# A hybrid encoder layer on one core: two query groups head by head, stick-breaking weights as differences, and masking inside a scan

## The chip, the cores and the metric

The kernel runs on one core of a Trainium2 chip. The time is the device time of one execution in microseconds (us); before the change it is 2670.81 us, the median of three runs from 2665.74 to 2673.22. Engines are called as in the profile: PE (TensorE, with PEld for its weight loads), DVE (VectorE), ACT (ScalarE), POOL (GpSimd) and SP, whose queue starts nearly all DMA transfers.

## The reference

One layer: an RMS norm with scale and shift, one input projection, two kinds of attention with eight heads of 64 channels each, an output projection, and an MLP of 1024 x 4096 with a squared ReLU. The sequence has 2048 positions, the model 1024 channels, all float32. The change touches the stick-breaking heads most:

```python
z = jnp.einsum('bqhd,bkhd->bhqk', qb, kb).astype(jnp.float32) * scale
strict = s_idx < t_idx
log_beta = jax.nn.log_sigmoid(z)
log_1m_beta = jnp.where(strict, jax.nn.log_sigmoid(-z), 0.0)
suffix = lax.cumsum(log_1m_beta, axis=3, reverse=True) - log_1m_beta
w = jnp.where(strict, jnp.exp(log_beta + suffix), 0.0)
out = jnp.einsum('bhqk,bkhd->bqhd', w.astype(v.dtype), vb)
```

So the weight of a key is sigmoid(z) times the product of sigmoid(-z) over all keys between it and the query. The other eight heads are a softmax over the query's chunk of 64 and the eight chunks before it, with a relative bias:

```python
s = jnp.einsum('bnqhd,bnkhd->bnhqk', qc, k_band) * (d ** -0.5) + bias[None, None]
p = jax.nn.softmax(jnp.where(valid[None, :, None, None, :], s, NEG_INF), axis=-1)
```

## The kernel before

The sequence is reversed on the host, so that a key before a query stands to its right and the product over keys runs from left to right. Positions are cut into four blocks of 512, numbered 0 to 3; block 3 holds the earliest positions. Nearly all matrices are split into a high and a low part of float32r, and a product is made of two or three matmuls of these.

There are three stages. The first, some 420 us, normalizes and projects what the attention needs first, and puts q, k and v into DRAM scratch. The last, from about 1370 us, is the end of the output projection and the MLP. Between them lies the attention stage. It is a list of *units* (`units`), each of four steps. A unit `SB(h, g, c)` is stick-breaking head h, query block g, key block c; it is *diagonal* where c == g. A unit `CA(h, g)` is softmax head h of query block g, with up to 1024 keys. A *group* is all that has one g. Before the change the list goes group by group: 3, 2, 1, 0, in each first all SB units, then all CA units.

In the loop over `steps`, step i holds for its front unit `soft1` (and `soft2`), for the unit eight steps back (`LAG`) the transposes of its weights, their split into `wth` and `wtl`, and the product with the values; then the scores of step i + 1; and then `fill`, which spends credit on matmuls of dense work, the *fillers*: the projection of block 1 (`fill_qkv`, tiles pf, weights fw), that of block 0 (its activations fx come from `scr_h`), and the output projections of finished groups (`outproj`, tiles po, weights ow). Order on PE, ACT, DVE and POOL is that of the program.

A stick-breaking step before the change: PE makes z (two matmuls) and in a diagonal unit adds a third, identity times `maskb`, which puts -1e30 where the key isn't strictly before the query. ACT takes sigmoid(z) into b, then sigmoid(-z) in place. DVE scans sigmoid(-z) to running products, into p, whose column 0 is the carry from the key block before. POOL multiplies b by p. Each p is held until the same query rows come again in the next key block, four steps later. In the softmax units DVE adds bias and reduces to the row's extreme (`CUSTOM_DVE_ANT_0 s`), ACT takes the exponential, POOL scales by the reciprocal sum (`cols`).

When a unit is done (`finish`), the two halves of its accumulator in PSUM (the products with the high and the low part of v) are summed: ACT copies one half to `otmp`, DVE adds the other into o; when both heads of a pair are there, `keep` splits o into `os` and stores it.

Loads stand on SP's one queue: a unit's q, k and bias two units ahead (`load`), its v two steps after its start (`load_values`). Weights of a filler's first piece are asked for when the filler begins, after its activation tiles; they lie in `ring`, which has three buffers of 1 MB. The PSUM pool pz has four banks for z, wt and the softmax scores together.

Of the kernel before, what the change touches and what calls it, by code (L numbers as in the profile page):

```python
# [9 lines left out]
F32 = mybir.dt.float32  # L10
# [8 lines left out]
P = 128  # L19
# [60 lines left out]
def encoder_kernel(ctx, tc, xT, c, g1, g2, w_in, w_rest, gqk, bias, w_o, w1, w2, w_ada, b_ada, out):  # L80
# [20 lines left out]
    def scratch(name, shape, *counts):  # L101
# [18 lines left out]
    pool.affine_select(  # L120
        out=maskb, in_=maskb, pattern=[[1, P]], base=0, channel_multiplier=-1,
        compare_op=ALU.is_gt, fill=NEG,
    )
    ones = cpool.tile([P, P], F32, name="ones")
# [531 lines left out]
    if True:  # L656
        kp0 = ph.enter_context(tc.tile_pool(name="kp0", bufs=3, side="right"))
        zp = ph.enter_context(tc.tile_pool(name="zp", bufs=6, side="right"))
        zw = ph.enter_context(tc.tile_pool(name="zw", bufs=12, side="right"))
        ppo = ctx.enter_context(tc.tile_pool(name="ppo", bufs=2, space=PSUM))  # L660
        ab = (ppo, "acc", 2)

        ldq = osp
# [90 lines left out]
        class SB(Unit):  # L754
# [10 lines left out]
            def load(self):  # L765
                if self.first:
                    pend["q"] = load_q(0, self.h, self.g)
                    pend["last"] = [None] * 4
                self.q = pend["q"]
                self.carry = pend["last"]  # L770
                self.k = load_k(0, self.h, self.c, 1, f"{self.g}_{self.c}")

            def load_values(self):
                self.v = load_v(0, self.h, self.c, 1, f"{self.g}_{self.c}")
# [12 lines left out]
            def soft1(self, qi):  # L787
                nm = f"{self.nm}_{qi}"
                c0 = qi * P if self.diag else 0
                n = TB - c0  # L790
                z = self.z
                b = zw.tile([P, TB], F32, tag="w", name=f"b{nm}")
                pt = zp.tile([P, TB + 1], F32, tag="p", name=f"p{nm}")
                act.activation(b[:, :n], z[:, :n], AF.Sigmoid, scale=0.125)
                act.activation(z[:, :n], z[:, :n], AF.Sigmoid, scale=-0.125)
                before = ones[:, 0:1] if self.diag else self.carry[qi]
                pool.tensor_copy(pt[:, 0:1], before)
                dve.tensor_tensor_scan(
                    pt[:, 1 : n + 1], z[:, :n], zero.to_broadcast([P, n]), 1.0 if self.diag else before,
                    op0=ALU.mult, op1=ALU.add,  # L800
                )
                pool.tensor_tensor(b[:, :n], b[:, :n], pt[:, :n], op=ALU.mult)
                self.carry[qi] = pt[:, n : n + 1]
                self.ws.append((b, c0))
# [8 lines left out]
        class CA(Unit):  # L813
# [9 lines left out]
            def load(self):  # L823
                h, g, nk = self.h, self.g, self.nk
                self.q = load_q(1, h, g)
                self.k = load_k(1, h, g, nk // TB, f"{g}")
                self.bt = op.tile([P, WIN], F32, tag="bias", name=f"bias{h}_{g}", bufs=2)
                sp.dma_start(self.bt, scr_b[h,])

            def load_values(self):  # L830
                self.v = load_v(1, self.h, self.g, self.nk // TB, f"{self.g}")

# [66 lines left out]
        class Filler:  # L899


            def __init__(self, make, *x):
                self.tiles = []
                self.gen = make(self, *x)
                self.src = next(self.gen)

            def fetch(self, n):
# [18 lines left out]
        def fill_qkv(self, tb, ht, pieces):  # L926

            self.tiles = ht or []
            yield None if ht else lambda k: scr_h[:, k]
            ht = self.moving()  # L930

            def load(piece, i):
# [3 lines left out]

            nxt = [load(pieces[0], i) for i in range(2)]
            yield "wait" if tb == 0 else "start"
            for n, piece in enumerate(pieces):
                grp, hf = divmod(piece, 2)  # L940
                w, nxt = nxt, []
                for j in range(2):
# [5 lines left out]
                    for tt in range(last + 1):  # L948
                        tl = slice((2 * j + tt) * P, (2 * j + tt + 1) * P)
                        for k in range(KT):  # L950
                            if n + 1 < len(pieces) and j and tt == last and k in (0, 4):
                                nxt.append(load(pieces[n + 1], k // 4))
                            wk = w[k // 4][:, k % 4]
# [20 lines left out]
        def outproj(self, g):  # L974
            yield lambda k: scr_m[g, k]

            def load(n):
                w = ring.tile([P, 2, KT, P], F32R, tag="r8", name=f"ow{g}_{n}")
                sp.dma_start(w.bitcast(F32), scr_wo[n,])
                return w  # L980

            mx = self.moving()
            ws = [load(0), load(1)]
            rx = load_residual(g, 0, xrp)
            yield "wait"
            for n in range(KT):
# [3 lines left out]
                if n + 2 < KT:  # L990
                    ws.append(load(n + 2))
                if n + 1 < KT:
                    rx = load_residual(g, n + 1, xrp)
                else:
                    yield "ahead"
# [59 lines left out]
        def fill(part):  # L1055
# [5 lines left out]
            while credit >= 1 and filler and not rest:  # L1061
                got = next(filler[0].gen, None)
                if got is None:
                    filler.pop(0)
                elif got == "ahead":
                    for f in filler[1:2]:
                        f.ahead()
                elif callable(got):
                    soon.append(got)
                    rest = 1  # L1070
                elif got in RESTS:
                    rest = RESTS[got]
                else:
                    credit -= got
                    work -= got
# [603 lines left out]
```

## Time and profile before

| what | before |
|---|---|
| runs, us | 2665.74, 2673.22, 2670.81 (median 2670.81) |
| the profiled execution | span 2672.1 us, first to last instruction; the page gives no other time of it |
| idle time of PE, 400 to 700 us | 24.1 us |
| idle time of PE, 700 to 1350 us | 17.4 us |
| idle time of PE, 1350 to 2650 us | 4.6 us |
| bytes moved by DMA | 651.28 MB |
| table loads on ACT | 8, 1.28 us each |

The profile is one execution, recorded by the hardware. Its page lists each engine's busy time; a group row names the engine, the operation, out<-in by the program's tile names, the count, then busy us and mean ns of one, then the idle time just before, and what ended it. PE's matmuls overlap: the length of one is not the time for which it holds the engine; that is seen from the start of the next. Other views cut the span into stretches, list who waited for whom, or show the instructions in order of time.

### The profile page before, as it was taken

How to read it: one execution, taken by the hardware profiler on the slowest of the kernel's cores; microseconds unless marked ns; L12 is line 12 of the kernel's file. 1: busy time of each engine (PE TensorE's matmuls, PEld its weight loads, DVE VectorE, ACT ScalarE, POOL GpSimd, SP SyncE). 2: the span in 40 equal slices, each digit the busy share in tenths (PEclk: the TensorE clock that was granted, in tenths of full speed). 3: DMA queues.
4: the chain of work that ended last, by engine and by line, in shares of the span. 5: the costliest groups of instructions: out<-in, count | busy, mean ns of one | idle time of the engine just before them, and what ended most of it. 6: DMA issues, size and time to landing. Idle time of an engine off the chain costs nothing. (4 is left out here: it accounts for less than half of the span.)

```text
span 2672.1 us, 40291 instructions
## 1 busy us (share of the span) xinstructions
PE 2598.4 (97%) x12944; PEld 2162.5 (81%) x12944; DVE 1929.1 (72%) x3287; ACT 1511.7 (57%) x2962; POOL 919.8 (34%) x1192
## 2 busy tenths in 40 slices
PE   6999999898999999999999999999999999999999
PEld 5888887687878887778788888878888888888887
DVE  7656766698789878989768787677857656555555
ACT  5333436787688878878654444456544545444443
POOL 4330144576467656767522323100002323200000
PEclk9999999999999999999999999999999999999999
DMA  9879888988887687756677777786675343465574
GB/s 339 307 300 363 313 318 261 262 255 258 251 260 249 203 260 251 236 191 206 208 276 274 273 255 266 252 322 221 222 265 175 138 166 140 148 250 197 194 266 156
DMA packets 263061, 651.28 MB, mean 244 GB/s; under 512 B 29632, under 2 KB 61376, under 8 KB 252992
## 3 DMA queue, kind: packets, MB, share of 16 engines
q1 hardware_dynamic: 261552, 643.98, 70.5%
q10 hardware_dynamic: 1296, 4.72, 0.4%
q8 instruction: 103, 1.69, 0.3%
q14 instruction: 110, 0.90, 0.1%
HBM read 457.21 MB, written 191.37 MB: 243 GB/s over the span
## 5 line engine op out<-in xcount | busy, mean ns | idle before, releaser
L42 PE MATMUL ps<-oph,opv 128*128 128x512 f32 x2688 | 612.5, 390 | 0.3
L42 PE MATMUL ps<-h,opw 128*128 128x512 f32 x2664 | 607.0, 390 | 4.3 <-DVE cx L42 4.3
L42 PEld LDWEIGHTS ps<-oph,opv 128*128 128x128 f32 x2688 | 503.8, 188 | 107.0 <-DVE opv L42 1.2
L42 PEld LDWEIGHTS ps<-h,opw 128*128 128x128 f32 x2664 | 500.6, 188 | 110.3 <-DVE cx L42 5.8
L42 POOL TENSOR_TENSOR b<-b,p 128x512 f32<-128x512 f32 (+1 forms) x320 | 360.3, 1126 | 197.9 <-DVE p L42 176.6
L42 DVE TENSOR_TENSOR wtl<-wt,wth 128x512 fp32r<-128x512 f32 (+3 forms) x544 | 290.5, 545 | 52.5 <-ACT wth L42 50.0
L42 ACT CAST wth<-wt 128x512 fp32r<-128x512 f32 (+3 forms) x544 | 257.8, 485 | 118.8 <-PE wt L42 104.0
L42 DVE TENSOR_TENSOR oph<-hw,oph 128x512 fp32r<-128x512 f32 x224 | 156.4, 698 | 220.4 <-ACT oph L42 220.4
L42 ACT CAST oph<-hw 128x512 fp32r<-128x512 f32 x224 | 139.5, 623 | 283.3 <-PE ps L42 267.2
L42 PE MATMUL pt<-w,ht 128*128 128x512 f32 x1248 | 288.7, 391 | 2.2 <-DVE qh L42 2.2
L42 POOL TENSOR_TENSOR ts<-w 128x512 f32<-128x512 f32 x32 | 44.8, 1400 | 668.4 <-DMA w<-in_w_dram 576.7
L42 PEld LDWEIGHTS pt<-w,ht 128*128 128x128 f32 x1248 | 232.8, 188 | 50.5 <-ACT csq L42 2.9
L42 DVE TENSOR_TENSOR_SCAN p<-z,p,zero 128x512 f32<-128x512 f32 x192 | 246.1, 1282 | 34.6 <-ACT z L42 29.2
L42 PE MATMUL acc<-wth,v 128*128 128x512 f32 (+3 forms) x544 | 222.6, 413 | 0.8 <-ACT wth L42 0.8
L42 ACT ACTIVATE b<-z 128x512 f32<-128x512 f32 (+1 forms) x320 | 171.7, 537 | 65.7 <-PE z L42 48.3
L42 PE MATMUL z<-k,q 128*128 128x512 f32 (+3 forms) x640 | 186.5, 373 | 9.7 <-DVE p L42 7.2
L42 POOL TENSOR_TENSOR e<-e,cols 128x640 f32<-128x640 f32 (+4 forms) x128 | 143.2, 1123 | 146.1 <-DVE cols L42 81.3
L42 PE MATMUL acc<-wtl,v 128*128 128x512 f32 (+3 forms) x544 | 187.1, 350 | 0.0
L42 DVE TENSOR_TENSOR opw<-w,opw 128x512 fp32r<-128x512 f32 x127 | 103.8, 819 | 113.1 <-ACT opw L42 113.0
L42 PE MATMUL wt<-ident,b 128*128 128x128 f32 x1088 | 173.3, 275 | 6.8 <-DVE cols L42 5.1
L42 ACT ACTIVATE z<-z 128x512 f32<-128x512 f32 (+1 forms) x320 | 170.4, 532 | 0.0
L42 PEld LDWEIGHTS wt<-ident,b 128*128 128x128 f32 x1088 | 134.8, 142 | 37.9 <-DVE cols L42 6.7
(193 smaller groups left out, 4257.6 us busy)
## 6 DMA issues: line engine op xcount, KB each, us to landing
hw<-scr_hid SPq DMA_DIRECT2D x112, 512.0 KB, 3.9
k<-scr_k SPq DMA_DIRECT2D x272, 128.0 KB, 4.2
v<-scr_v SPq DMA_DIRECT2D x136, 256.0 KB, 4.3
q<-scr_q SPq DMA_DIRECT2D x128, 256.0 KB, 5.4
w<-in_w_dram SPq DMA_DIRECT2D x64, 512.0 KB, 5.2
hw<-scr_s SPq DMA_DIRECT2D x64, 512.0 KB, 4.6
fw<-scr_w SPq DMA_DIRECT2D x28, 1024.0 KB, 7.0
wa<-in_w_ada_dram SPq DMA_DIRECT2D x48, 512.0 KB, 6.3
```

What stands on the lines that cost most here:

```text
L42: return lambda *x, **y: self.tc.keep_in_program_order(f(*x, **y))
```

## The change

- The units of groups 3 and 2 are mixed: for each head SB(h,2,2), SB(h,2,3), SB(h,3,3); then for each head CA(h,2), CA(h,3). Units that follow each other and use the same k and v share one load; CA(h,3) uses the second half of what CA(h,2) loaded, and its bias. Groups 1 and 0 follow as before.
- A stick-breaking weight is the difference of two neighbouring running products, p[i] - p[i+1], which is p[i] times sigmoid(z). ACT's sigmoid(z) goes.
- The mask matmul goes. In a diagonal unit the scan is max(z * state, held), where `held` is 1 at masked places and 0 elsewhere: the running product stays 1 there, and the difference is 0.
- `finish` copies both halves with ACT; when both heads of a pair are there, POOL adds the two tiles (`total`), and `keep` comes two steps after that.
- The first weights of the next filler are asked for in the last piece of the one before (`weight`). The pool of p has five buffers in place of six.

```diff
-    identb = cpool.tile([P, P], BF16, name="identb")
-    dve.tensor_copy(identb, ident)
-    maskb = cpool.tile([P, P], BF16, name="maskb")
-    pool.memset(maskb, 0.0)
...
-        zp = ph.enter_context(tc.tile_pool(name="zp", bufs=6, side="right"))
+        zp = ph.enter_context(tc.tile_pool(name="zp", bufs=5, side="right"))
...
+        held = kp0.tile([P, TB], F32, tag="held", name="held", bufs=1)
+        pool.memset(held, 0.0)
+        pool.affine_select(
+            out=held[:, :P], in_=held[:, :P], pattern=[[1, P]], base=0, channel_multiplier=-1,
+            compare_op=ALU.is_gt, fill=1.0,
+        )
...
-                pend["o"] = op.tile([P, TB], F32, tag="o", name=f"o{u.nm}")
-            o = pend["o"]
-            tmp = op.tile([P, TB], F32, tag="otmp", name=f"otmp{u.nm}")
+                pend["o", u.g] = [op.tile([P, TB], F32, tag=t, name=f"{t}{u.nm}") for t in ("o", "otmp")]
+            o, tmp = pend["o", u.g]
             act.copy(tmp[r : r + HD, :], u.acc[q : q + HD, :])
-            dve.tensor_tensor(o[r : r + HD, :], u.acc[r : r + HD, :], tmp[r : r + HD, :], op=ALU.add)
+            act.copy(o[r : r + HD, :], u.acc[r : r + HD, :])
             if u.h % 2:
-                soon.append(lambda: keep(u, o))
+                soon.append(lambda: total(u, o, tmp))
+
+        def total(u, o, tmp):
+
+            pool.tensor_tensor(o, o, tmp, op=ALU.add)
+            soon.append(lambda: soon.append(lambda: keep(u, o)))
...
-                self.k = load_k(0, self.h, self.c, 1, f"{self.g}_{self.c}")
+                if pend.get("k0") != (self.h, self.c):
+                    pend["k"] = load_k(0, self.h, self.c, 1, f"{self.g}_{self.c}")
+                    pend["k0"] = self.h, self.c
+                self.k = pend["k"]
...
-                pe.matmul(z[:, :n], self.q[:, 1, qs], self.k[:, c0:], start=False, stop=not self.diag)
-                if self.diag:
-                    pe.matmul(z[:, :P], identb, maskb, start=False, stop=True)
+                pe.matmul(z[:, :n], self.q[:, 1, qs], self.k[:, c0:], start=False, stop=True)
...
-                act.activation(b[:, :n], z[:, :n], AF.Sigmoid, scale=0.125)
                 act.activation(z[:, :n], z[:, :n], AF.Sigmoid, scale=-0.125)
                 before = ones[:, 0:1] if self.diag else self.carry[qi]
                 pool.tensor_copy(pt[:, 0:1], before)
...
+                if self.diag:
+                    dve.tensor_tensor_scan(pt[:, 1 : n + 1], z[:, :n], held[:, :n], 1.0, op0=ALU.mult, op1=ALU.max)
+                else:
+                    dve.tensor_tensor_scan(
+                        pt[:, 1 : n + 1], z[:, :n], zero.to_broadcast([P, n]), before, op0=ALU.mult, op1=ALU.add
+                    )
+                pool.tensor_tensor(b[:, :n], pt[:, :n], pt[:, 1 : n + 1], op=ALU.subtract)
...
+                if g == NTB - 1:
+                    self.k, self.bt = pend["wide"].k[:, TB:], pend["wide"].bt
+                    return
+                pend["wide"] = self
...
+            self.firsts = [lambda i=i: load(pieces[0], i) for i in range(2)]
...
+                            if j and tt == last and k in (0, 4):
+                                if n + 1 < len(pieces):
+                                    nxt.append(load(pieces[n + 1], k // 4))
+                                else:
+                                    yield "weight"
...
-        for g in range(NTB - 1, -1, -1):
+        for h in range(NH):
+            units += [SB(h, 2, 2), SB(h, 2, 3), SB(h, 3, 3)]
+        units += [CA(h, g) for h in range(NH) for g in (2, 3)]
+        for g in (1, 0):
...
+                elif got == "weight":
+                    for f in filler[1:2]:
+                        f.weight()
```

Three places show what this moves. The first is PE's queue in a diagonal step of head 3, group 2, query rows 1, before; `z_3_2_2_1` is the scores' bank, `pf` dense filler, `wt` the transposes of the unit eight steps back:

```order
L42 MATMUL acc_1_2_2_6036<-wtl_1_2_3_2_6081,v_1_2_3_5890 128x512
L42 MATMUL z_3_2_2_1_6177<-k_3_2_2_5944,q_3_2_5941 128x384 x2
L42 LDWEIGHTS identb
L42 MATMUL z_3_2_2_1_6177<-maskb,identb 128x128
L42 MATMUL pf_1_1_6093<-ht_4_2633,fw_1_1_5696 128x512 x3
L42 MATMUL wt_2_2_2_2_6186<-ident,b_2_2_2_0_5952 128x128
```

And the same step in the changed kernel:

```order
L42 MATMUL acc_2_2_2_4739<-wtl_2_2_2_2_4688,v_2_2_2_4500 128x384
L42 MATMUL z_3_2_2_1_4768<-k_3_2_2_4550,q_3_2_4547 128x384 x2
L42 MATMUL pf_3_1_4621<-ht_5_2627,fw_3_1_4255 128x512 x2
L42 MATMUL wt_2_2_3_2_4773<-ident,b_2_2_3_0_4558 128x128
L42 MATMUL wt_2_2_3_2_4773<-ident,b_2_2_3_1_4580 128x128
```

The load of the identity and the mask's matmul are gone; the filler follows on the scores. The second place is DVE's queue in the softmax heads of group 2, at the end of head 4, before (`ISA s` is the reduction with the bias, `ISA cols` the reading of its result):

```order
L42 RECIPROCAL cols<-cols 128x1
L42 TENSOR_TENSOR wtl_5_2_0_8453<-wt_5_2_0_8441,wth_5_2_0_8452 128x128
L42 TENSOR_TENSOR wtl_5_2_5_8457<-wt_5_2_5_8443,wth_5_2_5_8456 128x384
L42 TENSOR_TENSOR o_4_2_8462<-acc_4_2_8279,otmp_4_2_8463 64x512
L42 ISA s_7_2_3_8448,cols<-cz_7_2_3_8470,bias_2_8061,cols 128x512
L42 ISA cols 128x1
```

The corresponding rows of the changed kernel, at the end of head 5's transposes:

```order
L42 RECIPROCAL cols<-cols 128x1
L42 TENSOR_TENSOR wtl_5_2_0_7895<-wt_5_2_0_7883,wth_5_2_0_7894 128x128
L42 TENSOR_TENSOR wtl_5_2_5_7899<-wt_5_2_5_7885,wth_5_2_5_7898 128x384
L42 TENSOR_TENSOR stf_2_1_7908<-pf_2_1_7544,stf_2_1_7908 128x512
L42 ISA s_6_2_3_7890,cols<-cz_6_2_3_7916,bias_2_7557,cols 128x512
L42 ISA cols 128x1
```

The sum `o` no longer stands ahead of the reduction (`stf` is the end of a piece of filler, which happens to fall here). The third place is SP's queue where the projection of block 0 begins, before (fx are its activation tiles, fw its weights):

```order
L914 DMA fx_5_7418<-scr_h 128x1024
L914 DMA fx_6_7420<-scr_h 128x1024
L914 DMA fx_7_7422<-scr_h 128x1024
L934 DMA fw_2_0_7424<-scr_w_222 128x2048
L934 DMA fw_2_1_7426<-scr_w_222 128x2048
L670 DMA q_3_2_7458<-scr_q_2_1_101 64x1024 x2
```

In the changed kernel the first of these weights, fw_2_0, stands 21 rows further ahead, and the second here:

```order
L953 DMA fw_2_1_6968<-scr_w_222 128x2048
L668 DMA q_4_2_7047<-scr_q_2_2_102 64x1024 x2
L839 DMA bias_2_7055<-scr_b_244 128x640
L937 DMA fx_4_7126<-scr_h 128x1024
L937 DMA fx_5_7128<-scr_h 128x1024
L937 DMA fx_6_7130<-scr_h 128x1024
```

Both weights now stand ahead of the last four activation tiles.

More of the change, by code (lines that the diff above doesn't have):

```diff
@@ L902, in __init__, with weight, weights @@
             def __init__(self, make, *x):
-                self.tiles = []
+                self.tiles, self.firsts, self.got = [], [], []
                 self.gen = make(self, *x)
                 self.src = next(self.gen)
+            def weight(self):
+                if self.firsts:
+                    self.got.append(self.firsts.pop(0)())
+            def weights(self):
+                while self.firsts:
+                    self.weight()
+                return self.got
             def fetch(self, n):
@@ L935, in load @@
                 return w
-            nxt = [load(pieces[0], i) for i in range(2)]
+            self.tiles = ht or []
+            self.firsts = [lambda i=i: load(pieces[0], i) for i in range(2)]
+            yield None if ht else lambda k: scr_h[:, k]
+            ht = self.moving()
+            nxt = self.weights()
             yield "wait" if tb == 0 else "start"
@@ L974, in outproj @@
         def outproj(self, g):
-            yield lambda k: scr_m[g, k]
             def load(n):
@@ L980, in load @@
                 return w
+            self.firsts = [lambda n=n: load(n) for n in range(2)]
+            yield lambda k: scr_m[g, k]
             mx = self.moving()
-            ws = [load(0), load(1)]
+            ws = self.weights()
             rx = load_residual(g, 0, xrp)
```

26 lines of the change are left out of this document (10 added, 16 removed).

## The prediction

> **What bounds the kernel now.** I read the page first, then the busy time by stretch, then the list of waits, and last the timeline at two places. The page's head gives the engines over the whole span:
>
> ```profile
> span 2672.1 us, 40291 instructions
> PE 2598.4 (97%) x12944; PEld 2162.5 (81%) x12944; DVE 1929.1 (72%) x3287; ACT 1511.7 (57%) x2962; POOL 919.8 (34%) x1192
> ```
>
> TensorE is busy for 97%, so time can be won only by taking work from it or by filling its idle 74 us. The stretches (columns: length, then busy us of PE, weight load, DVE, ACT, POOL, the granted clock, the DMA share, GB/s) say where that idle time lies:
>
> ```profile
> 400.00:700.00 300.00, 275.86 (x1619) 230.65 (x1618) 224.81 (x482) 213.50 (x500) 169.81 (x257) 0.95 0.85 258
> 700.00:1350.00 650.00, 632.65 (x3783) 535.01 (x3781) 558.41 (x1056) 507.97 (x1066) 430.21 (x567) 0.99 0.73 229
> 1350.00:2650.00 1300.00, 1295.40 (x5748) 1070.24 (x5749) 871.79 (x1292) 625.48 (x1101) 203.95 (x145) 1.00 0.63 226
> 450.00:500.00 50.00, 43.23 (x250) 35.36 (x249) 36.62 (x100) 38.04 (x100) 29.31 (x46) 0.93 0.97 286
> 500.00:550.00 50.00, 44.62 (x255) 36.43 (x255) 38.01 (x99) 39.55 (x101) 29.28 (x45) 0.96 0.94 276
> 650.00:700.00 50.00, 42.81 (x232) 35.42 (x231) 32.55 (x115) 30.05 (x66) 21.79 (x18) 0.90 0.87 264
> 800.00:850.00 50.00, 49.99 (x313) 43.11 (x312) 45.70 (x57) 41.53 (x85) 34.87 (x54) 1.00 0.83 256
> 1100.00:1150.00 50.00, 46.20 (x249) 36.83 (x248) 42.33 (x54) 37.83 (x75) 38.02 (x57) 0.97 0.77 245
> ```
>
> The first 400 us (projections) and everything after 1350 us (the MLP) are not touched. The attention stage is. Its first 300 us (groups 3 and 2) leave PE idle for 300 - 275.9 = 24.1 us, its last 650 us (groups 1 and 0) for 17.4 us. The idle time comes in lumps: 6.8, 5.4 and 7.2 us in three slices of 50, none at 800. In the same slices the granted clock falls (0.93, 0.96, 0.90), and DMA is nearly full in the first two. What PE waited for, over the whole run (total us, times, longest):
>
> ```profile
> PE wt L42 <- DVE cols L42: 9.3, 6, 2.5
> PE z L42 <- DVE p L42: 7.2, 11, 2.3
> PE cz L42 <- DVE cols L42: 6.2, 9, 1.8
> PE pf L42 <- DMA fw<-scr_w: 5.7, 2, 3.8
> PE cz L42 <- DMA k<-scr_k: 5.6, 3, 2.6
> ```
>
> So two kinds of wait carry it: late loads (k of the softmax heads, fw of the dense filler: 11.3 us, all before 680 us), and a DVE that is late (22.7 us).
>
> **The mask (removed from PE).** 128 matmuls of the mask go. Their group and the timeline around one (start, length, engine):
>
> ```profile
> L42 PE MATMUL z<-maskb,identb 128*128 128x128 bf16 x128 | 29.6, 231 | 0.0
> 859.91 0.23 PE L42 MATMUL z<-maskb,identb 128*128 128x128 bf16 x1
> 859.95 0.36 PE L42 MATMUL pf<-fw,fx 128*128 128x256 f32 x1
> ```
>
> Each lasts 231 ns, but matmuls are pipelined: the next one starts 0.04 us later. Bounds: 0 to 29.6 us; I take 128 x 0.04 = **5 us**, the issue step, because PE is held for that alone. The scan takes the masking over with an operand `held`; the trace has no scan with a full second operand and `max`. Nearest rows, with the operations that the other edits touch:
>
> ```profile
> L42 DVE TENSOR_TENSOR_SCAN p<-z,zero 128x512 f32<-128x512 f32 (+3 forms) x128 | 104.3, 818 | 20.3 <-ACT z L42 16.9 <-PE z L42 1.2 <-issue 1.1
> L42 DVE TENSOR_TENSOR_SCAN p<-z,p,zero 128x512 f32<-128x512 f32 x192 | 246.1, 1282 | 34.6 <-ACT z L42 29.2 <-POOL p L42 1.7 <-POOL b L42 0.8
> L42 DVE TENSOR_TENSOR wtl<-wt,wth 128x512 fp32r<-128x512 f32 x280 | 186.4, 673 | 30.8 <-ACT wth L42 30.3
> L42 POOL TENSOR_TENSOR b<-b,p 128x512 f32<-128x512 f32 x224 | 289.5, 1292 | 179.5 <-DVE p L42 164.7 <-DVE cols L42 9.9 <-DMA k<-scr_k 0.8
> L42 ACT ACTIVATE b<-z 128x512 f32<-128x512 f32 (+1 forms) x320 | 171.7, 537 | 65.7 <-PE z L42 48.3 <-POOL p L42 8.3 <-POOL b L42 3.9
> L42 DVE TENSOR_TENSOR o<-acc,otmp 64x512 f32<-64x512 f32 x64 | 44.0, 687 | 28.5 <-ACT otmp L42 28.1
> L42 ACT COPY otmp<-acc 64x512 f32<-64x512 f32 x64 | 37.2, 582 | 2.8 <-PE acc L42 1.3
> ```
>
> A scan's 1282 ns is twice the 673 ns of an ordinary two-operand DVE operation of that size, so the recurrence and not the reading of a second operand looks like its limit: I take no change for the 128 diagonal scans; bounds -0 and +104 us (doubled), the latter a rival below.
>
> **Weights as differences.** 320 sigmoids leave ACT (171.7 us). ACT was never the bound, so this is nothing by itself; but each stood ahead of the sigmoid that the scan needs, so the scan can start about 0.5 us earlier and release the PSUM bank of z sooner. POOL's subtraction has two 128x512 operands like the multiplication before: 1292 ns, bounds 0.2 us either way, hidden while POOL is idle about a third of the stage (430 of 650 us busy). One p buffer fewer (5): a step needs its own and the four whose last column the next block reads, which is five; the sixth had only been slack, and what frees the oldest (the next block's scan) comes a step before. I cost it at nothing, with 2 us of bank waits at worst. `held` itself is a memset and a select on POOL before the first diagonal scan: nothing.
>
> **Sums on GpSimd.** 64 DVE additions go (44.0 us), and with them 28.1 us in which DVE stood waiting for ACT's copy with the next work queued behind. ACT gets 64 copies of 0.58 (37 us, less than what it lost), POOL 32 additions of 128x512 (32 x 1.29 = 41 us). What an addition does where it stands, at the end of group 2's softmax heads:
>
> ```profile
> 736.56 0.58 ACT L42 COPY otmp<-acc 64x512 f32<-64x512 f32 x1
> 737.18 0.68 DVE L42 TENSOR_TENSOR o<-acc,otmp 64x512 f32<-64x512 f32 x1 [0.87 <-ACT otmp L42]
> 737.78 0.73 DVE L42 CUSTOM_DVE_ANT_0 s<-cz,bias,cols 128x512 f32<-128x512 f32 x1
> 738.62 0.83 ACT L42 ACTIVATE e<-s,cols 128x640 f32<-128x640 f32 x1 [0.91 <-DVE cols L42]
> 738.77 1.26 POOL L42 TENSOR_TENSOR e<-e,cols 128x640 f32<-128x640 f32 x1 [2.45 <-DVE cols L42]
> ```
>
> DVE idles 0.87 us, adds for 0.68, and only then reduces the next scores; the exponential and the scaling are late, and PE's 2.5 us wait of wt on DVE cols lies there. The new rows have that reduction without the sum ahead of it. Of the 22.7 us of waits on DVE some 16 lie after 700 us or at the switches that stay; I take **6 us** from 17.4 (bounds 0 and 12). The new wait is POOL's, on ACT's two copies; behind it stand the next carry copy and subtraction, whose reader, the transposes, comes eight steps later.
>
> **Groups 3 and 2 together, shared loads, early weights.** 32 issues of k, 16 of v and 8 of bias go, of these:
>
> ```profile
> k<-scr_k SPq DMA_DIRECT2D x272, 128.0 KB, 4.2
> v<-scr_v SPq DMA_DIRECT2D x136, 256.0 KB, 4.3
> fw<-scr_w SPq DMA_DIRECT2D x28, 1024.0 KB, 7.0
> SPq L828 <- DVE cols L42: 26.2, 17, 3.4
> ```
>
> That is 32 x 128 + 16 x 256 + 8 x 320 = 10.8 MB, nearly all from the stretch of 300 us whose DMA runs at 258 GB/s: some 40 us of transfer less there. SP stood behind the bias load, waiting for its buffer, 17 times (the last row, from SP's own waits), and k for the next unit stands behind it; now one bias and one k serve two units. I take the 5.6 us of k as gone. The first weights of group 0's projection were asked for after its eight activation tiles; now both stand ahead of the last four. The longest wait of all, 3.8 us, goes; the four tiles (2 MB) remain beside the loads of the softmax heads, for which I leave 1 us. With the two-block order there are also two switches fewer between the attentions, and each short unit of group 3 stands beside a long one of group 2, so the DVE waits among the first 24.1 us are halved: 11.3 - 1 from loads, 6 from DVE, **16 us** (bounds 5.6 and 24.1). The dense filler keeps its rows; only how many stand in one piece differs.
>
> **The clock.** In the stretch 400 to 700 us the clock's shortfall is 0.05 x 300 = 15 us. Three slices hold (0.07 + 0.04 + 0.10) x 50 = 10.5 of it, those with the lumps. With the waits gone I take two thirds back, **7 us** (bounds 0 and 13). The Trainium skill (TensorE: Matmul & The Clock Gate, section "What's actually happening") lets the clock fall after at least one idle window of about 3.4 us. By that rule only the wait of 3.8 us would drop it, and this term would be some 2 us and the forecast 2642; here the rows differ, for the slices at 450 and 1100 hold no PE wait over 2.6 us and show 0.93 and 0.97.
>
> **Sum.** 5 + 6 + 16 + 7 = 34 us of 2672. The page gives no time beyond its span; 2672.1 lies among the runs (2665.7 to 2673.2), 1.3 above their median, so I subtract from the median: 2671 - 34 = **2637 us**.
>
> **The rivals.**
> - *The waits only move* (12%): with k and fw in time, DVE, busy 45.7 of 50 us at 800, ends last everywhere, and idle time as large stands elsewhere. Only the mask's 5 us remain: 2666. For it: the last row of 50 (1100) has 3.8 us idle that no part of this touches. Against: the slice at 800 loses 0.01 us with a DVE just as full.
> - *Every wait goes* (12%): 5 + 24.1 + 17.4 + 13 = 60 us: 2611. Against: switches between the attentions remain.
> - *The diagonal scans are slower* (5%, the other side): the one mechanism that I see for a loss. A diagonal scan that reads `held` takes twice as long, +104 us on DVE. At 800, where one unit in three is diagonal, a slice has two such units, 8 x 0.82 = 6.5 us more against 4.3 us of DVE's slack, so it decides from about two thirds longer; with half of it exposed, 2637 + 52 = 2689.
> - *POOL is late* (3%): each addition (1.29 us) shows in full, 32 x 1.29 = 41 us, 2637 + 41 = 2678, which with a little more is a loss. It decides once POOL falls eight steps behind; a full step costs DVE 1.28 + 0.67 = 1.95 us and POOL 1.29, so an addition is made good in two steps. The Trainium skill (GPSIMD Engine Reference, section "4.1 Engine selection") says to put elementwise additions on VectorE, GpSimd being some two times slower; the trace agrees on the ratio (1292 to 673 ns).
> - *The early weights aren't early* (6%): the ring has three buffers, and if the second waits for one until the projection begins, the 3.8 us and their clock stay: 2643.
>
> **How the numbers follow.** The forecast has 62%. The range leaves out the first, third and fourth rival (20%): down to 2611 less 2, up to 2662, where only the mask, the k loads and half of their clock are won. About 0.3% (8 us) is what a measurement of this kernel can tell from no change. Faster by more: 62 + 12 + 6 = 80%; within: 12%; slower: 5 + 3 = 8%.
>
> **What would show it.** No wait of PE on k or fw before 680 us; the clock at 0.97 or more in all slices of 400 to 700, PE idle there under 10 us; no mask group; diagonal scans still 0.82 us in the mean; ACT near 1375 us, DVE near 1885, POOL near 961 busy; the transposes' waits on DVE cols down by half. I am wrong if PE's idle time in the stage stays near 41 us, or if DVE's scans grow.

## The result, and the profile after

The changed kernel takes 2623.02 us (median of four runs, 2620.22 to 2625.26); the kernel before takes 2668.27 us (median of four runs, 2664.34 to 2673.22, three of them those of the table above). The ratio is 0.983, with a 95% interval of 0.9815 to 0.9845: 45 us less. The forecast was 34 us less and 2637 us, in a range of 2609 to 2662.

The head of the page after, one of the four runs (2620.22 us, the shortest, while the profiled execution of before lies near the top of its own runs; so the two spans differ by 54 us where the medians differ by 45):

```profile
span 2618.2 us, 39617 instructions
PE 2565.2 (98%) x12816; PEld 2153.3 (82%) x12816; DVE 1881.5 (72%) x3222; ACT 1408.0 (54%) x2704; POOL 896.3 (34%) x1224
```

DVE is where the prediction put it (1885). ACT was to fall to 1375 and fell to 1408: the two sigmoids of a step had overlapped on ACT (in the rows further below the second starts 0.49 us after a first that lasts 0.60), so taking one away frees less than its length. POOL was to rise to 961 and fell to 896, for a reason that its group row shows below. The stretches, with the columns of before:

```profile
400.00:700.00 300.00, 289.53 (x1750) 250.70 (x1749) 230.45 (x541) 210.01 (x480) 182.45 (x282) 0.99 0.81 251
700.00:1350.00 650.00, 637.46 (x3780) 547.54 (x3779) 539.30 (x994) 431.85 (x877) 396.81 (x582) 1.00 0.74 238
450.00:500.00 50.00, 48.99 (x281) 41.04 (x279) 41.38 (x62) 35.00 (x75) 32.92 (x63) 1.00 0.78 238
500.00:550.00 50.00, 49.08 (x277) 41.14 (x277) 42.92 (x62) 34.13 (x72) 33.12 (x64) 1.00 0.81 246
1100.00:1150.00 50.00, 50.00 (x279) 41.97 (x278) 45.72 (x58) 30.79 (x58) 32.27 (x55) 1.00 0.73 237
```

PE's idle time is 10.5 us in the first stretch (24.1 before) and 12.5 us in the second (17.4). What the clock costs is its shortfall times the length of the stretch. Its column is rounded, so it is better added up from slices of 25 us. In the changed kernel one slice of each stretch shows 0.93 and all others 1.00: 0.07 x 25 = 1.75 us in each. Before, the slices from 425, 475, 500, 600, 625 and 650 us fall short by 0.07, 0.13, 0.07, 0.04, 0.03 and 0.20, which is 13.5 us in the first stretch, and those from 1000 and 1125 by 0.07 each, which is 3.5 us in the second. The lumps at 450, 500 and 1100 are gone. The last 30 us of the second stretch already belong to the stage behind, since the attention stage ends at 1319 us (at 1370 before, by the last matmul into an accumulator). What PE still waits for in the attention stage, longest in total first:

```profile
PE wt L42 <- DVE cols L42: 6.2, 5, 2.3
PE z L42 <- DVE p L42: 5.9, 10, 1.9
PE cz L42 <- DVE wtl L42: 4.2, 5, 2.0
PE cz L42 <- DVE cols L42: 2.9, 4, 0.9
```

No wait on k or fw is left, and nearly all that remains is on DVE. The groups that the change touches (out<-in, count, then busy us and mean ns, then idle before):

```profile
L42 POOL TENSOR_TENSOR b<-p 128x512 f32<-128x512 f32 x224 | 233.1, 1040 | 197.1 <-DVE p L42 120.5 <-PE z L42 34.8 <-PE wt L42 20.3
L42 DVE TENSOR_TENSOR_SCAN p<-z,p,zero 128x512 f32<-128x512 f32 x192 | 245.6, 1280 | 29.8 <-ACT z L42 24.1 <-POOL p L42 5.0
L42 DVE TENSOR_TENSOR_SCAN p<-z,held 128x512 f32<-128x512 f32 (+3 forms) x128 | 104.1, 815 | 28.0 <-ACT z L42 26.8 <-POOL b L42 1.1
L42 POOL TENSOR_TENSOR o<-o,otmp 128x512 f32<-128x512 f32 x32 | 41.2, 1288 | 7.1 <-ACT o L42 7.1
```

The diagonal scans with `held` last 815 ns against 818 without it: no change, as taken. POOL's subtraction of two views of one tile lasts 1040 ns where the multiplication of two tiles lasted 1292.

So the gain came, and 11 us more of it than forecast, and the two traces don't say which edit won what. The experiments part them. Each is timed against the kernel before on the same chip (its medians were 2667.5, 2669.2 and 2669.0 us in the three sets), and its ratio is to be held against 0.983. What an edit is worth is the difference of two such ratios times 2669 us; the intervals are about 0.0013 to each side, so such a difference holds to some 5 us. Of the diffs below only the lines that matter are shown; dots mark what is left out.

### The profile page after: what moved, and what is told of

It reads as the page before. It is cut to its first block, busy times and chain, and to the rows that moved or that the text cites. A ratio compares the mean times of both kernels' runs of the same rounds, so it can differ in the third digit from the quotient of the medians.

```text
span 2618.2 us, 39617 instructions
## 1 busy us (share of the span) xinstructions
PE 2565.2 (98%) x12816; PEld 2153.3 (82%) x12816; DVE 1881.5 (72%) x3222; ACT 1408.0 (54%) x2704; POOL 896.3 (34%) x1224
## 5 line engine op out<-in xcount | busy, mean ns | idle before, releaser
L42 POOL TENSOR_TENSOR b<-p 128x512 f32<-128x512 f32 (+1 forms) x320 | 291.9, 912 | 219.5 <-DVE p L42 129.6
L42 DVE TENSOR_TENSOR wtl<-wt,wth 128x512 fp32r<-128x512 f32 (+3 forms) x544 | 290.6, 545 | 65.0 <-ACT wth L42 62.7
L42 DVE TENSOR_TENSOR_SCAN p<-z,p,zero 128x512 f32<-128x512 f32 x192 | 245.6, 1280 | 29.8 <-ACT z L42 24.1
L42 PE MATMUL po<-fx,ow 128*128 128x512 f32 x576 | 160.3, 393 | 0.0
```

The costliest lines, as they stand in the source:

```text
L42: return lambda *x, **y: self.tc.keep_in_program_order(f(*x, **y))
```

## Experiments: one edit taken back at a time

**The mask back on PE.** The changed kernel, with the third matmul of a diagonal step again and its scan without `held`.

```diff
+                if self.diag:
+                    pe.matmul(z[:, :P], identb, maskb, start=False, stop=True)
...
-                    dve.tensor_tensor_scan(pt[:, 1 : n + 1], z[:, :n], held[:, :n], 1.0, op0=ALU.mult, op1=ALU.max)
...
```

> The changed kernel with the mask again a third matmul into the scores (and the scan without held). Theory A: a mask matmul holds PE for 0.04 us until the next start and lengthens the interval behind it from 0.23 to 0.31 us, as the trace of before shows, so 128 x 0.12 = 15.5 us come back: about 2638.5 us. Theory B, the prediction's term: only the 0.04 us count, 5 us: 2628 us, and the surplus over the forecast lies elsewhere.

2627.53 us, ratio 0.9849 (0.9837 to 0.9862): 5 us above the changed kernel. The two intervals overlap, so by this run alone the mask could cost nothing. The run does speak against 0.12 us for each of the 128, which is theory A.

**The sigmoid and the product back.** ACT makes sigmoid(z) first again, POOL multiplies.

```diff
+                act.activation(b[:, :n], z[:, :n], AF.Sigmoid, scale=0.125)
                 act.activation(z[:, :n], z[:, :n], AF.Sigmoid, scale=-0.125)
...
-                pool.tensor_tensor(b[:, :n], pt[:, :n], pt[:, 1 : n + 1], op=ALU.subtract)
+                pool.tensor_tensor(b[:, :n], b[:, :n], pt[:, :n], op=ALU.mult)
```

> The changed kernel with ACT's sigmoid(z) and POOL's multiplication again (masked keys keep a weight here, since the product isn't a difference). Theory A: ACT has room (418 of 650 us busy after), so only the scan's start 0.5 us later counts: 2 to 5 us more, 2625 to 2628. Theory B: the surplus over the forecast comes from here, ACT's relief and POOL's shorter subtraction (0.91 against 1.13 us in the mean): 10 us more or above, 2633.

2651.04 us, ratio 0.9935 (0.9921 to 0.9948): 28 us above. This is the largest single part of the gain, and the prediction had put it at nothing. In its list of waits and its stretches:

```profile
PE z L42 <- DVE p L42: 18.5, 31, 2.3
...
400.00:700.00 300.00, 281.81 (x1671) 241.38 (x1669) 220.10 (x498) 234.05 (x549) 192.44 (x273) 0.99 0.77 241
700.00:1350.00 650.00, 629.61 (x3736) 536.60 (x3735) 536.30 (x1015) 526.48 (x1111) 454.29 (x589) 0.99 0.71 226
```

PE stands 31 times (10 in the changed kernel) for a bank of z that the scan has not yet released: 18.5 us against 5.9. Idle time is 7.7 and 7.9 us more in the two stretches. ACT has 95 us more to do in the second stretch (526 of 650) and is still less busy than DVE (536). So ACT's busy time didn't become the bound. A longer chain in each step is the likelier cause; the second group of experiments takes this up.

**The sums back on DVE.**

```diff
-            act.copy(o[r : r + HD, :], u.acc[r : r + HD, :])
+            dve.tensor_tensor(o[r : r + HD, :], u.acc[r : r + HD, :], tmp[r : r + HD, :], op=ALU.add)
...
```

> The changed kernel with the two halves of a head's result summed on DVE again, behind ACT's copy. Theory A, as predicted: 6 us more, 2629, with PE's waits on DVE cols up. Theory B: DVE's waiting was hidden once ACT is free and its copy comes at once: within 2 us of 2623.

2623.27 us, ratio 0.9831 (0.9818 to 0.9843): no difference. Some waits shorten and others lengthen:

```profile
PE wt L42 <- DVE cols L42: 6.9, 6, 1.8
PE cz L42 <- DVE cols L42: 5.2, 8, 1.1
PE z L42 <- DVE p L42: 4.5, 6, 1.9
```

**The old order with its own loads.** Groups one after the other; every unit loads its k, v and bias; the early weights stay.

```diff
...
-        for h in range(NH):
-            units += [SB(h, 2, 2), SB(h, 2, 3), SB(h, 3, 3)]
-        units += [CA(h, g) for h in range(NH) for g in (2, 3)]
-        for g in (1, 0):
+        for g in range(NTB - 1, -1, -1):
```

> The changed kernel with groups 3 and 2 one after the other again, each unit with its own loads; early weights stay. Theory A, as predicted: PE's waits on k and on DVE between 400 and 700 us come back, some 12 us, and with them the half-rate clock, 7 or more: 2640 to 2645. Theory B: the loads are hidden once ACT and DVE are lighter: at most 5 us, 2628.

2633.3 us, ratio 0.9871 (0.9858 to 0.9884): 11 us above, between the two theories. Waits on k come back:

```profile
PE cz L42 <- DMA k<-scr_k: 3.2, 1, 3.2
...
PE z L42 <- DMA k<-scr_k: 2.0, 2, 1.5
```

What of this is the order and what the loads, the next one parts.

**The new order with its own loads.**

```diff
-                if pend.get("k0") != (self.h, self.c):
+                if True:
...
-                if g == NTB - 1:
-                    self.k, self.bt = pend["wide"].k[:, TB:], pend["wide"].bt
-                    return
...
```

> The changed kernel in its own order, but every unit loads its own k, v and bias again (24 more sets of loads); early weights, differences, mask by the scan and sums on GpSimd stay. It parts the 10 us that the order and the shared loads are worth together. Theory A (the loads carry it: with twice the transfers of the short heads SP and the queue are late again): PE waits on k of 5 us or more come back before 700 us with half-rate clock beside them, and the time is 2630 to 2634. Theory B (the order carries it: a short head beside a long one and two switches fewer): no such wait, 2621 to 2626.

2649.69 us, ratio 0.9927 (0.9912 to 0.9942): 26 us above the changed kernel, and 15 above the old order with loads of its own. Both expectations missed the size. Sharing is worth 26 us here, and the order by itself costs 15: it pays only because it lets loads be shared. The stretch of the softmax heads, first of this kernel:

```profile
575.00:600.00 25.00, 21.57 (x156) 19.83 (x155) 16.98 (x55) 16.44 (x38) 11.08 (x16) 1.00 1.05 306
600.00:700.00 100.00, 80.49 (x485) 71.58 (x484) 57.37 (x214) 64.37 (x160) 50.76 (x49) 0.90 0.88 267
```

and of the changed kernel:

```profile
575.00:600.00 25.00, 24.25 (x178) 22.79 (x177) 19.47 (x65) 19.12 (x44) 13.57 (x17) 1.00 1.03 293
600.00:700.00 100.00, 94.48 (x605) 83.12 (x605) 72.38 (x275) 81.31 (x205) 62.35 (x62) 0.98 0.81 255
```

PE is idle for 2.7 + 14.0 us more there, and the clock falls short by 8 us more: 25 of the 26. How one such gap comes about is seen on SP's queue of the kernel with its own loads, around head 3's short unit (start, length, what is loaded), with PE's first matmul of that unit:

```profile
656.51 0.80 SPq L685 DMA_DIRECT2D v<-scr_v  x2
657.40 0.38 SPq L712 DMA_DIRECT2D scr_m<-os  x1
658.16 1.65 SPq L668 DMA_DIRECT2D q<-scr_q  x2
660.59 1.69 SPq L676 DMA_DIRECT2D k<-scr_k  x2
667.16 1.22 PE L42 MATMUL cz<-k,q 128*128 128x512 f32 x2 [8.52 <-DVE wtl L42]
```

PE was ready at 658.6. The k that it needed was issued from 660.6 on, behind a v, a store and a q, and PE went on 4.9 us after the last of these issues ended (k takes 4.2 us in the median from issue to landing here, 11.6 at most). The releaser named, DVE's wtl, had long been done. A short unit takes 7.0 us in the mean in the changed kernel and a long one 9.1 (from the starts of their first scores), so the loads that SP puts out beside a short one have less time; with shared loads a short unit needs only a q. That this is why the order is dear is read from these rows; no run isolates it.

**The early weights taken back.**

```diff
                 elif got == "weight":
-                    for f in filler[1:2]:
-                        f.weight()
+                    pass
```

> The changed kernel with the first weights of group 0's projection asked for when that projection begins, not ahead of group 1's last tiles; all else stays. The prediction's step (the wait of 3.8 us on fw and its clock come back): 2628 to 2631, with PE waits pf on fw of 3 us or more. Rival (with the shared loads the queue has room, so the weights come in time anyhow): 2621 to 2625, no wait on fw over 1 us.

2620.86 us, ratio 0.9818 (0.9802 to 0.9833): no loss, and no wait on fw at all. With the shared loads the weights come in time even when they are asked for late. Whether asking early is worth something without shared loads was not tried.

## Experiments: why the differences were worth 28 us

Taking back the differences changes three things: ACT's work, its order, and POOL's operation. Two kernels were meant to part them, and a third puts the idea alone into the kernel before.

**An idle sigmoid ahead.** The changed kernel with a sigmoid(z) into b that POOL's difference overwrites.

```diff
+                act.activation(b[:, :n], z[:, :n], AF.Sigmoid, scale=0.125)
                 act.activation(z[:, :n], z[:, :n], AF.Sigmoid, scale=-0.125)
```

> The changed kernel with ACT's sigmoid(z) into b ahead of the one that the scan needs, as before, but with the weights still POOL's difference (b is overwritten). It tells apart what in the run with the multiplication cost 28 us. Theory A, ACT's order: z reaches the scan 0.5 us later and its PSUM bank is free later, PE waits for it: about 2643 to 2650. Theory B, POOL: the multiplication (1.29 against 1.04 us) held the p buffers: within 5 us of 2623.

2646.88 us, ratio 0.9915 (0.9901 to 0.9928): 23 of the 28 us, with POOL's cheaper subtraction still there. So ACT's part carries most of it; the 5 us left for POOL's operation are no more than such a difference can tell. The wait of PE is back as well:

```profile
PE z L42 <- DVE p L42: 16.4, 29, 1.9
```

The idle sigmoid makes the chain from scores to scan longer, and it also gives ACT more to do (527 of 650 us in the second stretch, 432 in the changed kernel). No run has the one without the other. The waits speak for the chain: DVE stands 68.7 us for the sigmoid that the scan needs, 50.9 in the changed kernel, while its wait for ACT's other work of a step, the copy `wth`, stays (61.7 and 62.7 us).

**The other factor made behind.** ACT makes 1 - sigmoid(-z) after the sigmoid that the scan needs; POOL multiplies.

```diff
                 act.activation(z[:, :n], z[:, :n], AF.Sigmoid, scale=-0.125)
+                act.activation(b[:, :n], z[:, :n], AF.Identity, scale=-1.0, bias=ones[:, 0:1])
...
-                pool.tensor_tensor(b[:, :n], pt[:, :n], pt[:, 1 : n + 1], op=ALU.subtract)
+                pool.tensor_tensor(b[:, :n], b[:, :n], pt[:, :n], op=ALU.mult)
```

> The changed kernel with the multiplication on POOL again, its factor 1 - sigmoid(-z) made by ACT behind the sigmoid that the scan needs (masked keys keep a weight here). ACT and POOL are as busy as in the run with the multiplication, but the scan isn't delayed. Theory A, ACT's order: within 8 us of 2623. Theory B, POOL's longer operation or ACT's busy time as such: 2643 to 2650.

2668.01 us, ratio 0.9996 (0.9987 to 1.0006): 44 us above, worse than with the extra work in front, and neither expectation's number. PE's wait for the bank is longer still:

```profile
PE z L42 <- DVE p L42: 29.5, 41, 2.3
```

The rows of one step say why. Before the change (PE's scores, ACT's two sigmoids, DVE's scan):

```profile
804.38 0.63 PE L42 MATMUL z<-k,q 128*128 128x512 f32 x2
805.11 0.60 ACT L42 ACTIVATE b<-z 128x512 f32<-128x512 f32 x1 [0.35 <-POOL p L42]
805.60 0.59 ACT L42 ACTIVATE z<-z 128x512 f32<-128x512 f32 x1
806.30 1.28 DVE L42 TENSOR_TENSOR_SCAN p<-z,p,zero 128x512 f32<-128x512 f32 x1 [0.19 <-ACT z L42]
```

The changed kernel:

```profile
788.32 0.62 PE L42 MATMUL z<-k,q 128*128 128x512 f32 x2
788.99 0.58 ACT L42 ACTIVATE z<-z 128x512 f32<-128x512 f32 x1 [0.28 <-PE z L42]
789.66 1.28 DVE L42 TENSOR_TENSOR_SCAN p<-z,p,zero 128x512 f32<-128x512 f32 x1
```

And with the other factor behind:

```profile
800.54 0.63 PE L42 MATMUL z<-k,q 128*128 128x512 f32 x2
801.21 0.58 ACT L42 ACTIVATE z<-z 128x512 f32<-128x512 f32 x1 [0.22 <-PE z L42]
801.88 0.69 ACT L42 ACTIVATE b<-z,ones 128x512 f32<-128x512 f32 x1
802.66 1.28 DVE L42 TENSOR_TENSOR_SCAN p<-z,p,zero 128x512 f32<-128x512 f32 x1 [0.20 <-ACT b L42]
```

From the scores to the scan's start it is 1.92, 1.34 and 2.12 us. In the third kernel the scan starts not 0.09 us after the sigmoid but 0.09 us after ACT's second read of the same bank: the program's wait of each of the 320 scans is for the count that this second activation reaches. So the reorder did not put the work behind the scan at all, and this kernel does not test ACT's busy time apart from the chain, as it was meant to. Over all 320 steps, the median time from the start of the second matmul of z to the end of the scan, worked out from the rows of each trace, orders these kernels by their time: 2.40 us in the changed kernel (2623), 2.96 with the idle sigmoid in front (2647), 3.17 with the factor behind (2668). It does so only where the other edits are the same: the kernel before has 2.97 us and takes 2668.

**The differences alone in the kernel before.**

```diff
-                act.activation(b[:, :n], z[:, :n], AF.Sigmoid, scale=0.125)
...
-                pool.tensor_tensor(b[:, :n], b[:, :n], pt[:, :n], op=ALU.mult)
+                pool.tensor_tensor(b[:, :n], pt[:, :n], pt[:, 1 : n + 1], op=ALU.subtract)
```

> The kernel before with the differences alone (one sigmoid and the subtraction; mask matmul, order, sums, loads as before). If the edit's worth is the same alone as in the whole, 28 us less than before: 2640. If it is worth this much only beside the other edits (five p buffers, POOL's additions): 5 to 12 us less, 2655 to 2662.

2658.16 us, ratio 0.9954 (0.9942 to 0.9967): 12 us won, where the same edit is worth 28 in the changed kernel, although the median step is 2.40 us here too. The wait that the edit shortens is small in the kernel before: PE's wait of z on DVE p falls from 7.2 to 3.9 us, where beside the other edits it falls from 18.5 to 5.9. And the late loads are still there:

```profile
PE cz L42 <- DMA k<-scr_k: 7.8, 3, 3.4
PE pf L42 <- DMA fw<-scr_w: 7.1, 2, 6.0
```

All other edits without the differences win 17 us (0.9935), the differences without the others 12, together they win 45: 16 us belong to the pair. A step that runs ahead waits for k or fw all the same, and loads in time help little where the scan is late; that reading fits the lists of waits, but no run isolates it. The kernel that wins 17 us leaves out the masking of the weights.

**The scan's input in SBUF.** The changed kernel, with ACT writing the sigmoid to b, so that z's bank could be free right after ACT's read.

```diff
-                act.activation(z[:, :n], z[:, :n], AF.Sigmoid, scale=-0.125)
+                act.activation(b[:, :n], z[:, :n], AF.Sigmoid, scale=-0.125)
...
-                        pt[:, 1 : n + 1], z[:, :n], zero.to_broadcast([P, n]), before, op0=ALU.mult, op1=ALU.add
+                        pt[:, 1 : n + 1], b[:, :n], zero.to_broadcast([P, n]), before, op0=ALU.mult, op1=ALU.add
```

> The changed kernel with ACT's sigmoid(-z) written to b in SBUF in place of z in PSUM, the scan reading b. The bank of z is then free when ACT is done, not after the scan. Theory A: PE's waits of z on DVE p (5.9 us) and shorter ones go: 2612 to 2618. Theory B, from the rule of the Trainium skill (SBUF - State Buffer, section "SBUF: two separate sides") that a DVE operation with two SBUF inputs and a GpSimd operation lock each other out: scans or subtractions grow by up to their overlap, 2630 or more.

2714.22 us, ratio 1.017 (1.0157 to 1.0184): 91 us above. The instructions that write p in this kernel (durations in ns: least, median, most), and one step of it:

```profile
L42 DVE TENSOR_TENSOR_SCAN p<-b,p,zero x192: 1254/1765/2408, 425.2 to 1312.6; 128x512 f32<-128x512 f32 x192
L42 POOL COPY p<-p x192: 178/1115/1127, 428.1 to 1313.3; 128x1 f32<-128x1 f32 x192
...
800.34 1.04 POOL L42 TENSOR_TENSOR b<-p 128x512 f32<-128x512 f32 x1 [0.17 <-DVE p L42]
800.71 1.76 DVE L42 TENSOR_TENSOR_SCAN p<-b,p,zero 128x512 f32<-128x512 f32 x1
801.33 1.11 POOL L42 COPY p<-p 128x1 f32<-128x1 f32 x1
```

The same rows of the changed kernel, whose scan reads z from PSUM:

```profile
L42 DVE TENSOR_TENSOR_SCAN p<-z,p,zero x192: 1256/1283/1289, 424.6 to 1222.4; 128x512 f32<-128x512 f32 x192
L42 POOL COPY p<-p x192: 178/183/191, 426.5 to 1223.0; 128x1 f32<-128x1 f32 x192
```

The shortest scan takes 1254 ns, as good as in the changed kernel (1256); one that starts while POOL subtracts ends 1.09 us after the subtraction's end (at 801.38), and the one-column copy that starts during the scan lasts until the scan's end (801.33 + 1.11 = 802.44; the scan ends at 802.47). The two engines go nearly in turns. The Trainium skill (SBUF — State Buffer, section "SBUF: two separate sides") says just that of a VectorE operation with two SBUF inputs beside a GpSimd operation that reads SBUF: whichever starts first has the shared ports for the whole instruction. The trace agrees in the main (1.09 us behind the subtraction's end is a little less than the 1254 ns of the shortest scan), and with z in PSUM the effect isn't there.

## Two more

**The mask alone in the kernel before.** The opposite of the first experiment.

```diff
-                if self.diag:
-                    pe.matmul(z[:, :P], identb, maskb, start=False, stop=True)
...
+                if self.diag:
+                    dve.tensor_tensor_scan(pt[:, 1 : n + 1], z[:, :n], held[:, :n], 1.0, op0=ALU.mult, op1=ALU.max)
```

> The kernel of before with the mask alone moved into the scan (no mask matmul; scans of the diagonal blocks with the held operand; five z banks of slack in p as in the change). Masked keys keep a weight here, so this leaves out the masking of the weights. The prediction's term, 0.04 us for each of 128: 2662 to 2666 beside a before of about 2669. Rival (the mask matmul also lengthens its follower, 0.12 us each in the trace): 2652 to 2656. Third (DVE's order decides there, so PE's freed time is only waited out): no change, 2667 or more.

2662.21 us, ratio 0.9979 (0.997 to 0.9989): 5.6 us won. The whole interval lies below 1, so this is a gain, and with the 5 us of the other side the term holds in both surroundings. This kernel has the five p buffers too, so no cost of the sixth one's loss shows here; it was not tested by itself.

**A blocked DVE queue.** An attempt at a faster kernel: the product `ndgm` of the second norm waits at the head of DVE's queue for POOL. In the changed kernel:

```profile
1096.34 0.69 DVE L42 TENSOR_TENSOR ndgm<-ident,nym 128x512 f32<-128x512 f32 x1 [2.27 <-POOL nym L42]
```

```diff
...
-                dg = norm_rstd(op, dense, rows[g], f"m{g}")
-                later.add(5, lambda: third(dg))
+                spread = norm_rstd(op, dense, rows[g], f"m{g}", split=True)
+                later.add(3, lambda: later.add(4, lambda dg=spread(): third(dg)))
```

> The changed kernel with one step of the second norm's row apart: the DVE product ndgm, which stands 2.27 us at the head of DVE's queue waiting for GpSimd's five small operations of the rsqrt, is issued three steps later, when its operand is there. In the trace of the changed kernel two such places cost PE 1.9 and 1.8 us of waits (z on DVE p, wt on DVE cols). Theory A (the blocked DVE queue makes those waits): both go, PE waits on DVE fall by 3 to 5 us, 2617 to 2621. Rival (DVE is late there anyway, with 90 of 100 us busy): the waits move, within 2 us of 2623.

2622.17 us (2617.03 to 2626.78), ratio 0.9823 (0.9806 to 0.9839): no difference that this measurement can tell. The waits did get shorter in its trace (z on DVE p 5.9 to 3.9 us, wt on cols 6.2 to 4.4), but 4 us of waits are within what the runs of one kernel differ by. No version tried beats the changed kernel beyond that.

## Why the prediction was right, and where it was not

The bound was read rightly: PE waits in lumps for late loads and for DVE, the clock falls with the lumps, and both come back. Idle time in the stage fell by 13.6 + 4.9 = 18.5 us where 16 + 6 were forecast; the clock gave 11.75 + 1.75 = 13.5 us where 7 were. With the mask's 5 this makes 37 us, of 45 between the medians and 54 between the two profiled executions; these views don't show where the rest lies. Edit by edit the forecast fits worse than in its total: 28 us come from an edit that was priced at nothing, while two others, forecast at 6 and 16 us without the clock, gave 0 and 11 with it. That the total came within the range is partly luck. Step by step:

- *The mask, 5 us*: 5 by taking it back, 5.6 by putting it in alone. Right, as is the choice of the issue step over the 231 ns.
- *`held` scans, no change*: 815 to 818 ns. Right; the rival of doubled scans fell. The limit on its other side was nearer than thought: scans that read z's values from SBUF and not from PSUM cost 91 us.
- *Weights as differences, "nothing by itself"*: the step that failed. The prediction saw that the scan starts about 0.5 us earlier (0.57 in the median step) and releases the bank sooner, and then priced that at nothing because ACT is not the bound. It is worth 28 us here. 23 of them come from the sigmoid ahead on ACT: with it back PE waits 16.4 us, not 5.9, for the bank that the chain from scores to scan holds. That its place in the chain and not its 95 us of ACT's time does this is read from the waits, not isolated. That POOL's subtraction lasts as long as the multiplication was wrong too: 1040 ns.
- *Sums on GpSimd, 6 us*: 0. The waits on DVE that were put down to the additions went with the other edits, or moved: without this edit they are as long in sum.
- *Groups 3 and 2, shared loads, early weights, 16 us*: 11 by taking back order and sharing together, their clock included. Within it the reasons were off: the order alone costs 15 us, sharing brings 26, and the early weights nothing. "Each short unit stands beside a long one" is no relief where loads aren't shared: k is late there. The waits on k and fw went as said, fw's without its own edit.
- *The clock, 7 us*: too low. In the first stretch 11.75 of 13.5 us came back, more than "two thirds" of the three slices that were counted, and half of the 3.5 us in the second, which the prediction left out. By the rule of the Trainium skill (TensorE: Matmul & The Clock Gate, section "What's actually happening") it would have been 2 us; the runs stand against that use of it.
- *The range*: its upper end doesn't follow from what it names. The mask and the k loads alone make 5 + 5.6 us, so 2660 before any clock, not 2662. The measured time is far from that end.

Of the signs named, the waits on k and fw, the clock in slices of 50 us (0.97 or more), the mask group, the scans' mean and DVE's busy time came as said; ACT's and POOL's busy time did not. PE's idle time from 400 to 700 us is 10.5, not under 10. The transposes' waits on DVE cols fell by a third, not by half. The removals sum to 28 + 5 + 0 + 11 = 44 of the 45 us, but the sum is no proof: put alone into the kernel before, the differences win only 12.

## What to carry to other kernels

An engine that is far from its bound can still cost time by its place in a chain: ask of each operation removed what starts earlier, and who waits for what that holds, before it is priced at nothing. An order of work and the loads that it needs are one thing: measured apart, the order here was a loss and the sharing more than the whole gain. And edits to two waits on one engine don't add up, so one taken out of the finished kernel and one put alone into the old one answer different questions.

## What was not expected of the hardware

- GpSimd's subtraction of two shifted views of one 128x512 tile takes 1040 ns; its multiplication or addition of two tiles of that size 1288 to 1292.
- A scan with both inputs in SBUF and GpSimd's operations go nearly in turns (1254 to 2408 ns for the scan, 183 to 1115 for a copy of one column); with one input in PSUM neither is lengthened.
- A second reader on ACT of the bank that the scan reads held the scan back by its whole length, by the wait that the program sets; nothing in the source asks for that order.
- The granted clock falls to 0.93 in slices of 25 us where the changed kernel's PE has no wait over 2.3 us (625 to 650 and 700 to 725, below). In the trace's record of the clock it falls to half for 3.41 us at a time. The changed kernel has three such falls ahead of its last 3 us (the third near 1701 us). Right before them stand stretches of the same length in which PE was idle for 47, 70 and 51%, in waits of at most 2.3 us; but one such stretch with 52%, near 1237 us, has no fall behind it.

```profile
625.00:650.00 25.00, 21.67 (x128) 17.93 (x127) 16.00 (x61) 18.52 (x46) 14.23 (x16) 0.93 0.83 259
700.00:725.00 25.00, 21.44 (x121) 17.91 (x120) 15.88 (x40) 19.00 (x45) 14.36 (x21) 0.93 0.78 234
```
